# Matmul with batch normalization: the last tile's statistics aggregated in two steps, and its last chunk computed by two halves of rows

## The chip, the cores and the metric

One core of one Trainium2 chip. The metric is device time in microseconds (us), median of several executions. An execution more than 1.5% above the fastest one of the same kernel counts as slow and is left out.

## The reference, cut to what matters

```python
batch, m, k, n = 16, 512, 1024, 768          # x: (16, 512, 1024), weight: (1024, 768), float32
y = np.matmul(x, weight)
mean = np.mean(y, axis=(0, 1), keepdims=True)
var = np.var(y, axis=(0, 1), keepdims=True)
return (gamma * (y - mean) / np.sqrt(var + eps) + beta).astype(np.float32)
```

Every output column needs its mean and variance over all 8192 rows before any of it can be stored. The kernel splits the 768 columns into six tiles of 128 (nt) and the rows into 16 chunks of 512 (c). Tile 5 is the last. The "hole" below is the pause of about a microsecond between the last stores of tile 4 and the first of tile 5, in which the DMA engines, which carry the stores, have little to do.

## The kernel before

The pools, in the order in which they are laid out in on-chip memory (SBUF).

```python
singles = ctx.enter_context(tc.tile_pool(name="singles", bufs=1))
xtpool = ctx.enter_context(tc.tile_pool(name="xtpool", bufs=C - EARLY))      # xT tiles, at the end o_sb tiles
ypool = ctx.enter_context(tc.tile_pool(name="ypool", bufs=C + (NT - GA) * 2 + 1))
sqpool = ctx.enter_context(tc.tile_pool(name="sqpool", bufs=4))
# ... cut: ring, w_sb and others in singles
stats = singles.tile([P, NT, C, 6], f32)
msq = singles.tile([P, GA], f32)
mv = singles.tile([P, NT, 2], f32)
# ... cut: std, tmp, rstd, warm
```

The end of a tile: statistics of each chunk, one aggregation, scale and shift, then for each chunk normalize, transpose, copy out of PSUM, store.

```python
def bn(nt, c):
    i = c if nt >= GA else COLS.index(c)
    seq(nc.vector.bn_stats(stats[:, nt, i, :], py[nt, c]))

def finish(nt):
    one = slice(nt, nt + 1)
    seq(nc.vector.bn_aggr(mv[:, nt, :], stats[:, nt, :, :]))
    seq(nc.scalar.activation(std[:, one], mv[:, nt, 1:2], AF.Sqrt, bias=eps_sb, scale=1.0))
    # ... cut: tmp, rstd, scale, shift

def out_copy(nts, m0, eng, late=False):
    # ... cut
    if late:                                     # the last tile only
        o_sb = xtpool.tile([P, tiles, cols], f32, tag="xT")
    else:
        o_sb = piece(tiles * cols).rearrange("p (s n) -> p s n", n=cols)     # a piece of ring
    # ... cut

def store(nts, m0, tiles):                       # rows of 128 floats: 512 bytes each
    seq(nc.sync.dma_start(out_flat[m0:m0 + tiles * P, nts[0] * P:(nts[-1] + 1) * P].rearrange(
        "(s p) n -> p s n", p=P), ost.pop((nts, m0))))
```

`at(time, function, ...)` only puts the functions into an order. Each engine then runs its own list in that order.

## Time and profile before

| | before |
|---|---|
| time, median of 6 | 221.13 us (220.65 to 222.17) |
| span of the profiled execution | 218.9 us |
| last chunk's first matmul | 197.94 us |
| square root (statistics done) | 201.14 us |
| first store of tile 5 issued | 203.72 us |
| last store landed | 217.41 us |

The chain and the statistics' durations are in the prediction below.

From the timeline of the DMA queue that issues the stores, the second store of tile 5 (start, length):

```profile
204.21 1.13 SPq L358 DMA_DIRECT2D out_dram<-o_sb  x1
```

Its issue takes 1.13 us, where the later ones take about 0.53.

### The profile page before, as it was taken

Reading aid. Unit: us, or ns where it says so; the run is one execution under the profiler, and the core shown is the slowest. Engines: PE = TensorE matmul, PEld = TensorE weight load, DVE = VectorE, ACT = ScalarE, POOL = GpSimd, SP = SyncE. Lnnn points to the kernel's source line nnn. Section 1 sums busy time; section 2 is a strip of 40 time slices with the busy share of each in tenths; the row PEclk is TensorE's granted clock in tenths of the full one; section 3 lists DMA queues with packets and bytes.
Section 4 is the critical chain, followed back from the end, with each engine's and each line's share of the span. In section 5 each row is a group of like instructions: output and inputs, shape, how many; then the busy total and the mean of one; then the engine's idle time right before and its main releaser. Section 6 shows DMA issues by size and latency. Waiting matters only on the chain.

```text
span 218.9 us, 3417 instructions
## 1 busy us (share of the span) xinstructions
PE 198.5 (91%) x1154; PEld 105.2 (48%) x1170; DVE 155.7 (71%) x264; ACT 119.8 (55%) x220; POOL 134.0 (61%) x153
## 2 busy tenths in 40 slices
PE   7998999999999999999999979999999988995900
PEld 3453545454544555546555534444444545651900
DVE  3223788897978789998554287889989999745800
ACT  2001454554543566636666225776676887985850
POOL 8897595977765799935559103999899953000000
PEclk9999999999999999999999999999999999999795
DMA  5999999999999999990000000986769899999698
GB/s 60 175 204 190 194 196 196 197 196 196 194 191 197 195 196 196 198 189 10 0 4 0 0 0 14 340 308 257 269 258 360 295 353 334 346 346 347 201 345 244
DMA packets 70161, 43.75 MB, mean 200 GB/s; under 512 B 4096, under 2 KB 69632, under 8 KB 70144
## 3 DMA queue, kind: packets, MB, share of 16 engines
q0 software_dynamic: 34624, 18.36, 61.1%
q1 hardware_dynamic: 35520, 25.18, 35.7%
q8 instruction: 9, 0.15, 0.3%
q14 instruction: 8, 0.07, 0.1%
HBM read 36.71 MB, written 25.17 MB: 283 GB/s over the span
## 4 chain that ended last, share of the span: by engine, by line
PE 64%; DVE 10%; POOL 8%; DMA 6%; issue 4%; ACT 3%; ACTq 0%; DVEq 0%; POOLq 0%
PE y_ps L190 31%; PE y_ps L180 29%; POOL ring L280 6%; PE o_ps L340 3%; ACT o_sb L353 3%; DVE stats L299 3%; DMA w_sb<-in_weight_dram 3%; DVE ring L274 2%; DVE y_sb L324 2%; DMA ring<-in_x_dram 2%; POOL w_sb L143 2%; DMA out_dram<-ring 1%; POOL ring L156 1%; DVE mv L306 1%; PE a_ps L266 1%
## 5 line engine op out<-in xcount | busy, mean ns | idle before, releaser
L190 PE MATMUL y_ps<-xT_sb,w_sb 128*128 128x512 bf16 (+1 forms) x477 | 117.5, 381 | 2.6 <-DMA w_sb<-in_weight_dram 1.4
L190 PEld LDWEIGHTS <-w_sb 128*128 128x128 bf16 x492 | 46.7, 96 | 60.8 <-issue 3.1
L302 ACT CAST y_sb<-y_ps 128x512 bf16<-128x512 f32 x60 | 35.4, 590 | 53.3 <-DVE stats L299 51.4
L180 PE MATMUL y_ps<-w_sb,xT_sb 128*128 128x384 bf16 x384 | 63.4, 326 | 0.0
L299 DVE BATCH_NORM_STATS2 stats<-y_ps 128x6 f32<-128x512 f32 x60 | 40.6, 684 | 22.5 <-PE y_ps L190 22.3
L280 POOL TENSOR_TENSOR ring<-ring,sum 128x768 f32<-128x768 f32 x24 | 43.5, 1847 | 17.9 <-ACT sum L268 14.0
L156 POOL DMA_DIRECT2D ring<-in_x_dram x72 | 45.2, 633 | 11.7 <-DVE xT_sb L168 6.1
L180 PEld LDWEIGHTS <-xT_sb 128*128 128x128 bf16 x384 | 37.5, 98 | 25.6
L206 POOL TENSOR_TENSOR sum<-sum,sq_sb 128x384 f32<-128x384 f32 x38 | 38.0, 1000 | 18.0 <-ACT sq_sb L202 16.8
L168 DVE STREAM_TRANSPOSE xT_sb<-ring 128x1024 f32<-128x1024 f32 (+1 forms) x34 | 39.5, 1167 | 12.0 <-DMA ring<-in_x_dram 12.0
L340 PE MATMUL o_ps<-ident,y_sb 128*128 128x128 bf16 x240 | 37.3, 230 | 5.5 <-DVE y_sb L324 5.2
L209 DVE TENSOR_TENSOR sum<-y_ps,sum 128x384 f32<-128x384 f32 x48 | 26.1, 544 | 14.6 <-ACT sq_sb L202 13.8
L202 ACT ACTIVATE sq_sb<-y_ps 128x384 f32<-128x384 f32 x48 | 23.4, 492 | 14.9 <-PE y_ps L180 11.4
L215 ACT CAST y_sb<-y_ps 128x384 bf16<-128x384 f32 x48 | 22.9, 476 | 7.5 <-DVE sum L209 7.3
L353 ACT CAST ring<-o_ps 128x1024 f32<-128x1024 bf16 (+1 forms) x24 | 22.5, 960 | 4.9 <-PE o_ps L340 2.5
L340 PEld LDWEIGHTS <-y_sb 128*128 128x128 bf16 x240 | 20.6, 104 | 9.1 <-DVE y_sb L324 7.3
L274 DVE TENSOR_TENSOR ring<-y_sb,a_ps 128x768 f32<-128x768 bf16 x24 | 22.3, 938 | 0.2 <-PE a_ps L266 0.2
L324 DVE TENSOR_SCALAR y_sb<-y_sb,scale,shift 128x512 bf16<-128x512 bf16 x43 | 17.3, 457 | 0.0
L319 ACT ACTIVATE y_sb<-y_sb,shift,scale 128x512 bf16<-128x512 bf16 x17 | 13.3, 813 | 0.1
L149 PE MATMUL idle_ps<-idle_sb 128*128 128x512 bf16 x37 | 9.8, 429 | 1.2 <-DVE idle_sb L100 1.2
L353 ACT CAST o_sb<-o_ps 128x512 f32<-128x512 bf16 x16 | 7.9, 679 | 1.2 <-PE o_ps L340 1.2
L149 PEld LDWEIGHTS <-idle_sb 128*128 128x128 bf16 x38 | 4.0, 108 | 6.4 <-issue 1.9
(45 smaller groups left out, 35.9 us busy)
## 6 DMA issues: line engine op xcount, KB each, us to landing
ring<-in_x_dram POOLq DMA_DIRECT2D x56, 256.0 KB, 8.5
out_dram<-ring SPq DMA_DIRECT2D x32, 384.0 KB, 2.9
out_dram<-ring SPq DMA_DIRECT2D x16, 512.0 KB, 5.9
out_dram<-o_sb SPq DMA_DIRECT2D x16, 256.0 KB, 3.3
ring<-in_x_dram POOLq DMA_DIRECT2D x16, 128.0 KB, 5.2
w_sb<-in_weight_dram POOLq DMA_DIRECT2D x8, 96.0 KB, 4.6
w_sb<-in_weight_dram POOLq DMA_DIRECT2D x4, 192.0 KB, 5.4
gamma_sb<-in_gamma_dram SPq DMA_DIRECT2D x6, 0.5 KB, 4.8
```

What stands on the lines that cost most here:

```text
L156: seq(nc.gpsimd.dma_start(x_bf[32 * i:32 * i + 32], src[:, :, KQ * i:KQ * (i + 1)]))
L168: seq(nc.vector.transpose(dst[:, half, :, jw0:jw1], src[:, :, jw0:jw1]))
L180: seq(nc.tensor.matmul(y_ps, xT[c][:, jw, s * P:(s + 1) * P, e], w_sb[:, jw, e, 0:NA], start=(jw == 0 and e == 0), stop=(jw == JW - 1 and ...
L190: seq(nc.tensor.matmul(y_ps, w_sb[:, jw, e, nt * P:(nt + 1) * P], xT[c][:, jw, q0 * QR:q1 * QR, e], start=(jw == 0 and e == 0 and q0 == 0) ...
L206: seq(eng.tensor_add(acc, acc, py.pop(("sq", c, s))))
L209: seq(nc.vector.tensor_add(sum1, py["row", c, s][:, 0:NA], sum1))
L274: seq(nc.vector.tensor_mul(o_sb, yrow[c][:, s:s + 2], aff[0][:, None, :].to_broadcast([P, 2, NA]),))
L280: seq(nc.gpsimd.tensor_add(o_sb, o_sb, sum1[:, None, :].to_broadcast([P, 2, NA])))
L299: seq(nc.vector.bn_stats(stats[:, nt, i, :], py[nt, c]))
L302: seq(nc.scalar.copy(y(nt, c), py.pop((nt, c))))
L340: seq(nc.tensor.transpose(dst, src, ident))
L353: seq(nc.scalar.copy(o_sb, src))
```

## The change

Intent: shorten what stands between the last matmul and the first store of tile 5. The statistics of chunks 0 to 13 become one triple (count, mean, sum of squares) while TensorE still works. The last chunk is computed as two halves of 256 rows, so that the first half is measured while the second is computed.

```diff
     stats = singles.tile([P, NT, C, 6], f32)
+    fin = singles.tile([P, 21], f32)
     msq = singles.tile([P, GA], f32)
@@ (in bn)
+        if (nt, c) == (NT - 1, C - 2):
+            seq(nc.vector.bn_stats(fin[:, 3:9], py[nt, c]))
+            return
@@
+    def sum_up():
+        seq(nc.vector.memset(fin[:, 0:1], float((C - 2) * CH)))
+        seq(nc.vector.bn_aggr(fin[:, 1:3], stats[:, NT - 1, 0:C - 2, :]))
+        seq(nc.vector.tensor_scalar(
+            fin[:, 2:3], fin[:, 2:3], float((C - 2) * CH), None, op0=ALU.mult))
+
+    def mm_half(q):
+        y_ps = psum.tile([P, CH], f32, tag="b")
+        py["half", q] = y_ps[:, 0:QR]
+        # ... cut: the 8 matmuls of mm, on 256 rows
+
+    def bn_half(q):
+        seq(nc.vector.bn_stats(fin[:, 9 + 6 * q:15 + 6 * q], py["half", q]))
+
+    def keep_half(q):
+        seq(nc.scalar.copy(y(NT - 1, C - 1)[:, q * QR:(q + 1) * QR], py.pop(("half", q))))
@@ (in finish)
-        seq(nc.vector.bn_aggr(mv[:, nt, :], stats[:, nt, :, :]))
+        src = stats[:, nt, :, :] if nt < NT - 1 else fin
+        seq(nc.vector.bn_aggr(mv[:, nt, :], src))
@@ (in the loop that orders the chunks)
+            if (nt, c) == (NT - 1, C - 1):
+                for q in range(QPC):
+                    at(pe, mm_half, q)
+                    pe += 0.9
+                    at(pe + 0.2, bn_half, q)
+                    at(pe + (0.4 if q == 0 else 1.0), keep_half, q)
+                at(pe - 2.4, sum_up)
+                continue
```

## The prediction

> **What bounds the kernel now.** I began with the page's second part, the span in 40 slices, to see what is busy at the end, and then took each stretch by itself.
>
> ```profile
> PE   7998999999999999999999979999999988995900
> DVE  3223788897978789998554287889989999745800
> ACT  2001454554543566636666225776676887985850
> ...
> GB/s 60 175 204 190 194 196 196 197 196 196 194 191 197 195 196 196 198 189 10 0 4 0 0 0 14 340 308 257 269 258 360 295 353 334 346 346 347 201 345 244
> ```
>
> TensorE is full until about 200 us, then it dips once and is idle after some 208 us. From slice 26 on the output stores keep the DMA engines near 345 GB/s, with one hole, the 201 of slice 38. The change touches only the last 128 columns of the output (tile 5), of which nothing can be stored before their mean and variance are known. So the stretch to read is the hole, from 198 to 206 us. The chain of work that ended last gives it step by step (columns: start us, length us, what):
>
> ```profile
> 197.04 2.72 PE y_ps L190 x12
> 199.79 0.71 DVE stats L299
> 200.52 0.60 DVE mv L306
> 201.14 0.30 ACT std L307
> 201.47 0.17 DVE rstd L311
> 201.66 0.16 DVE scale L312
> 201.82 0.14 DVE shift L313
> 201.99 0.42 DVE y_sb L324
> 202.46 0.62 PE o_ps L340 x4
> 203.11 3.78 ACT o_sb L353 x8
> ```
>
> This is a serial tail: last matmul, statistics of the last chunk (0.71), aggregation of all 16 chunks (0.60), square root and three tiny operations, first normalization, four transposes, first copy out of PSUM. The first store of tile 5 is issued at 203.72 us in the timeline. Whatever shortens the front of this chain should bring the first store, and the 15 behind it, forward. After that the stores set the time: 16 of 256 KB are 4.19 MB, and at the 346 GB/s that the windows of 1 us show from 206 to 217 us they need 12.1 us; the copies on ScalarE come every 0.48 us, faster than a store's 0.76 us. The same windows show the DMA engines around the hole (columns: stretch, its length, busy time of each engine, granted TensorE clock, DMA share, GB/s):
>
> ```profile
> 201.00:202.00 1.00, 0.00 (x0) 0.00 (x0) 0.73 (x6) 0.77 (x2) 0.00 (x0) 1.00 1.15 346
> 202.00:203.00 1.00, 0.54 (x6) 0.54 (x7) 1.00 (x4) 0.00 (x0) 0.00 (x0) 0.65 0.83 250
> 203.00:204.00 1.00, 1.00 (x12) 1.00 (x11) 1.00 (x5) 0.89 (x2) 0.00 (x0) 0.50 0.16 39
> ```
>
> Tile 4's stores run out at about 202.7 us, so there is a whole microsecond with hardly a transfer before the first new store is issued. An earlier first store lands in an empty queue.
>
> **What the Trainium skill says.** "TensorE: Matmul & The Clock Gate", section "Back-to-back issue gap", gives a spacing of N/2.4 + 2.5 ns for one matmul of N columns behind another when the clock is full, and warns that weight loads can raise it for small N. The trace is near it: eight matmuls of 512 columns take 1.81 us here (197.94 to 199.75), 0.227 us each instead of 0.216. Matmuls of 256 columns are in this kernel already, in its first chunk; in the timeline they start at 13.35, 13.57, 13.80 and 14.03 us with two to a step, so 0.113 us each against a stated 0.109. Two halves cost what one whole costs. The same page, section "What's actually happening", has the array's clock halved after an idle window of about 3.4 us that runs freely. The trace agrees: the clock is 0.50 from 202.3 to 205.7 us, 3.4 us, after the pause of 2.71 us in PE. "VectorE: DVE Perf Modes", section "The TRN2 errata", makes an operation a fixed cost plus one cycle per element at 0.96 GHz. For the statistics this fits: 512 elements are 0.533 us, and 0.700 us are measured, a fixed 0.167 us. "PSUM — Partial Sum Buffer", section "PSUM bank collisions", says no two engines may use one bank at once; the halves get a bank each, so measuring the first need not stop the second's matmuls. No page gives a duration for the two batch-norm operations; those come from the trace.
>
> **The change part by part.** The aggregation is in the trace in two sizes (ns: least, median, most):
>
> ```profile
> L236 DVE BATCH_NORM_AGGREGATE mv<-stats x3: 205/205/245, 126.5 to 126.8; 128x2 f32<-128x24 f32 x3
> L306 DVE BATCH_NORM_AGGREGATE mv<-stats x3: 575/587/589, 150.9 to 200.5; 128x2 f32<-128x96 f32 x3
> L299 DVE BATCH_NORM_STATS2 stats<-y_ps x60: 652/688/700, 19.8 to 199.8; 128x6 f32<-128x512 f32 x60
> ```
>
> - Removed from the chain: the aggregation over 96 values. It becomes one over 21 (a triple for 14 chunks, two for chunk 14, two for each half). From (587 - 205)/(96 - 24) = 5.3 ns a value, 21 values are 205 - 3 x 5.3 = 189 ns. Saved: 587 - 189 = 0.40 us.
> - Removed from the chain: half of the last statistics. 256 fewer elements at 0.96 GHz, so 0.70 becomes 0.70 - 0.267 = 0.43 us. Saved: 0.27 us.
> - Moved: statistics of the first half. They run while TensorE computes the second half: ready at about 197.94 + 0.95 = 198.89 us, done at 199.32, and the second half ends at 199.79. Beside other work, cost nothing.
> - Added on TensorE: eight more matmuls, of half the width. 16 x 0.113 = 1.81 us, as before. Cost 0.0 us.
> - Added on VectorE, ahead of chunk 14's statistics: a memset of one column (59 ns for such a one), an aggregation over 84 values (205 + 60 x 5.3 = 523 ns) and a multiplication of one column (169 ns for a like one), 0.75 us and some 0.1 us between them. They stand in order after chunk 13's statistics (195.67 to 196.37) and before those of chunk 14 at 197.98; VectorE idled 1.61 us there waiting for TensorE. They fit, with 0.7 us over. Cost 0.
> - Added on ScalarE: one copy of 512 becomes two of 256. The first runs near 199.4 us, before the square root needs the engine at about 200.47; the second comes after the square root as the whole one did (201.34 to 201.90), and is done long before the first o_sb copy. Cost 0.
> - Not changed: square root to first copy, as many steps of the same size; 16 stores of the same size; everything before 195 us.
>
> Sum: 0.40 + 0.27 = 0.67 us. The square root should start at 201.14 - 0.67 = 200.47, the first o_sb copy at 202.44, the first store at 203.05, 0.35 us after the queue ran empty. The whole end then shifts by the same amount: 221.04 - 0.67 = 220.4 us, or 0.3%.
>
> **The rivals.**
> - The hole is filled by the transfers: tile 4's stores still occupy the queue when tile 5's arrive, so the earlier start is worth nothing. Against it are the 39 GB/s in 203 to 204 us and the queue's end at 202.7; the shift of 0.67 is smaller than the 1.0 us between that end and the first issue. If it were so, the time would stay at 221.0. A part of it may be true: the second store's issue took 1.13 us where the others took about 0.53, and if the issues are irregular in another way the gain could shrink or grow by 0.3 us.
> - Weight loads bind with narrow matmuls: 16 loads of 96 ns stand under 16 steps of 113 ns, with little room, and the skill's page warns of it. At 0.13 us a step the last chunk would take 2.08 us, 0.27 us more, which leaves 0.4 us: 220.6. Against it is the spacing of the 24 narrow matmuls at 13 us, which changed weights each time as well.
> - The aggregation has a larger fixed cost, or costs by the number of distinct statistics in some other way. Then only the half of the statistics is gained, 0.27 us: 220.8. The two sizes measured speak against it.
> - The clock: the pause in PE shrinks from 2.71 to about 2.04 us. The halved clock made the first four transposes last 0.62 us where four at full clock take about 0.4. If the shorter pause, or merely another position of the free-running window, keeps the clock, 0.2 us more are gained: 220.2. The window from 205.7 to 209.1 was 2.0 us busy of 3.4 and did not lower the clock; the one from 198.9 to 202.3 was 0.85 us busy and did. After the change the least busy window would hold 1.4 us. Between the two; I give it one in three, and later transposes don't matter, since the copies and then the stores are slower.
> - Slower: only if the new VectorE work delayed chunk 14's statistics, or a half waited for a bank. The eight tiles ahead of the second half's bank were freed more than a microsecond before, by the order of the program. I see no way past 0.3 us.
>
> **Range and chances.** The three times of before spread from 220.65 to 222.17, a longer tail above than below, which is larger than the effect. Mechanisms alone give 220.2 to 221.0; with a median's noise of some 0.4 us on both sides I take 219.7 to 221.3. Faster by over 2% would need 4.4 us, six times what the chain offers; slower by as much has no mechanism. Within 2%: 0.97.
>
> **What would show it.** In the profile after, right if: the last statistics are of 128x256 and last 0.43 us; the last aggregation is of 128x21 and lasts about 0.19 us; the square root starts about 0.65 us after the last statistics start (1.35 before); the last chunk's 16 matmuls take 1.8 us; the aggregation over 84 values ends before 197.5 us with chunk 14's statistics still waiting for TensorE; the first store is issued 5.1 us after the last chunk's first matmul (5.8 before); from there to the end of the span it stays 15.2 us. The prediction is wrong if that last length grows by what the first shrank, or if the statistics' two pieces are not shorter in proportion.

## More of the kernel before

Of the windows of before, here are one from the start of tile 5's stores and the stretch that is mostly stores (columns: stretch, its length, busy time and instructions of PE, PEld, DVE, ACT, POOL, granted TensorE clock, DMA share, GB/s):

```profile
204.00:205.00 1.00, 1.00 (x13) 1.00 (x11) 1.00 (x5) 1.00 (x3) 0.00 (x0) 0.50 0.40 120
...
208.00:217.00 9.00, 0.00 (x0) 0.00 (x0) 0.00 (x0) 3.04 (x7) 0.00 (x0) 0.75 1.15 345
```

In the first the stores have begun and move only 120 GB/s; the 345 GB/s at the end of the second line are the rate at which tile 5 leaves.

## The result, and the profile after

The changed kernel takes 223.15 us (median of 6, 222.83 to 223.74), before 221.13. The ratio is 1.0089, with a 95% interval of 1.0064 to 1.0114. A ratio here is the mean time of one kernel's fast runs over that of the other's fast runs of the same rounds, so not quite the ratio of the medians. The kernel became slower by 0.9%, where a gain of 0.3% was predicted. It stays within 2%, to which the prediction gave 0.97, but lies outside its range of 219.7 to 221.3 us.

The chain of work that ended last, of the changed kernel (start us, length us, what):

```profile
199.26 1.83 PE y_ps L317 x16
201.11 0.45 DVE fin L324
201.58 0.26 DVE mv L335
201.86 0.30 ACT std L336
...
202.71 0.43 DVE y_sb L353
203.18 0.41 PE o_ps L369 x4
203.62 3.97 ACT o_sb L382 x8
```

Count from the last chunk's first matmul, 199.26 us here and 197.94 before. The square root comes at 2.60 us for 3.20. The first o_sb copy comes at 4.36 for 5.17, and the first store is issued at 4.97 (204.23 us) for 5.78. The front of the chain is 0.8 us shorter, a little more than was predicted, but not for the predicted reason alone: 0.60 of it comes from the statistics (0.67 predicted), and 0.21 from the first four transposes, which found the clock full in this trace (0.41 us for 0.62). The instructions that write or read `fin` (columns: engine, operation, count: ns least/median/most, first and last start) show how:

```profile
L324 DVE BATCH_NORM_STATS2 fin<-y_ps x2: 433/433/433, 200.2 to 201.1; 128x6 f32<-128x256 f32 x2
...
L308 DVE BATCH_NORM_AGGREGATE fin<-stats x1: 534/534/534, 197.7 to 197.7; 128x2 f32<-128x84 f32 x1
...
L335 DVE BATCH_NORM_AGGREGATE mv<-fin x1: 249/249/249, 201.6 to 201.6; 128x2 f32<-128x21 f32 x1
```

So far the prediction holds. Now the windows of the changed kernel, at the start of the stores and in the stretch of stores alone:

```profile
203.00:204.00 1.00, 0.82 (x11) 0.62 (x12) 1.00 (x4) 0.38 (x1) 0.00 (x0) 1.00 1.15 348
204.00:205.00 1.00, 1.00 (x16) 0.71 (x13) 1.00 (x5) 1.00 (x3) 0.00 (x0) 1.00 0.56 167
205.00:206.00 1.00, 1.00 (x16) 0.70 (x13) 1.00 (x5) 1.00 (x3) 0.00 (x0) 1.00 0.87 258
...
208.00:217.00 9.00, 0.43 (x6) 0.23 (x4) 0.00 (x0) 3.55 (x8) 0.00 (x0) 0.72 0.99 288
```

The last column tells where the time went. Tile 4's stores still ran at 348 GB/s, but tile 5's run at 288 where before had 345. They are the same 16 stores of 256 KB with the same rows of 512 bytes. At 345 GB/s their 4.19 MB take 12.2 us, at 288 they take 14.6. The DMA share falls with the rate, from 1.15 to 0.99: the single packets last about as long (from 208 to 216 us 26.4 ns in the mean before, 27.3 now), but they follow each other more slowly. From the first store's issue to the end of the span it takes 17.2 us (204.23 to 221.47) in place of 15.2.

Two more differences are in the trace. The second store's issue, 1.13 us before, is short now:

```profile
204.72 0.44 SPq L387 DMA_DIRECT2D out_dram<-o_sb  x1
```

And a 16-KB packet on the DMA queue that the profile calls "q8 instruction" has moved. In before's packet records the last one starts at 203.6 us, in the hole. In the changed kernel it starts at 200.2 us, while tile 4's stores still fill the DMA engines. The DMA view of the changed kernel for 198 to 202 us has it, and that of before for the same stretch has none:

```profile
q1 hardware_dynamic: 2691, 1.35, 113.0%
q8 instruction: 1, 0.02, 1.5%
```

Last, the profiled execution was already 1.3 us later when the last chunk began. This part is no effect of the change that can be shown. The first statistics of the kernel start at 19.8 us in before's trace and at 20.9 in the changed kernel's, but two executions of one and the same kernel (after_moved below) have 21.3 and 19.5.

### The profile page after: what moved, and what is told of

Its sections match the earlier page's. It is cut to its first block, busy times and chain, and to the rows that moved or that the text cites. A ratio compares the mean times of both kernels' runs of the same rounds, so it can differ in the third digit from the quotient of the medians.

```text
span 221.5 us, 3438 instructions
## 1 busy us (share of the span) xinstructions
PE 199.8 (90%) x1162; PEld 105.0 (47%) x1178; DVE 156.3 (71%) x268; ACT 119.9 (54%) x221; POOL 134.4 (61%) x153
## 4 chain that ended last, share of the span: by engine, by line
PE 63%; DVE 10%; POOL 8%; DMA 6%; issue 4%; ACT 3%; ACTq 0%; DVEq 0%; POOLq 0%
PE y_ps L191 30%; PE y_ps L181 28%; POOL ring L281 6%; PE o_ps L369 3%; ACT o_sb L382 3%; DMA w_sb<-in_weight_dram 3%; DVE stats L303 2%; DMA ring<-in_x_dram 2%; DVE ring L275 2%; DVE y_sb L353 2%; POOL w_sb L144 2%; DMA out_dram<-ring 1%; POOL ring L157 1%; PE y_ps L317 1%; PE a_ps L267 1%
## 5 line engine op out<-in xcount | busy, mean ns | idle before, releaser
L191 PE MATMUL y_ps<-xT_sb,w_sb 128*128 128x512 bf16 (+1 forms) x469 | 115.8, 382 | 2.6 <-DMA w_sb<-in_weight_dram 1.6
L191 PEld LDWEIGHTS <-w_sb 128*128 128x128 bf16 x484 | 46.2, 96 | 59.4 <-issue 2.6
L330 ACT CAST y_sb<-y_ps 128x512 bf16<-128x512 f32 x59 | 34.8, 590 | 54.2 <-DVE stats L303 52.3
L303 DVE BATCH_NORM_STATS2 stats<-y_ps 128x6 f32<-128x512 f32 x58 | 39.2, 684 | 19.9 <-PE y_ps L191 19.7
L169 DVE STREAM_TRANSPOSE xT_sb<-ring 128x1024 f32<-128x1024 f32 (+1 forms) x34 | 39.5, 1168 | 13.6 <-DMA ring<-in_x_dram 13.5
L369 PEld LDWEIGHTS <-y_sb 128*128 128x128 bf16 x240 | 19.1, 97 | 9.7 <-DVE y_sb L353 6.5
L150 PE MATMUL idle_ps<-idle_sb 128*128 128x512 bf16 x37 | 11.2, 473 | 1.2 <-DVE idle_sb L100 1.2
```

Of the source, the lines that this page charges most:

```text
L169: seq(nc.vector.transpose(dst[:, half, :, jw0:jw1], src[:, :, jw0:jw1]))
L191: seq(nc.tensor.matmul(y_ps, w_sb[:, jw, e, nt * P:(nt + 1) * P], xT[c][:, jw, q0 * QR:q1 * QR, e], start=(jw == 0 and e == 0 and q0 == 0) ...
L330: seq(nc.scalar.copy(y(nt, c), py.pop((nt, c))))
L369: seq(nc.tensor.transpose(dst, src, ident))
```

## The experiments

**Theory.** `fin` takes 84 bytes, for which the layout gives 96: in the compiled program msq moves from 61728 to 61824, and everything behind it moves as far. The o_sb tiles, which lie in the pool behind singles, move from 61952, a multiple of 256, to 62048, 96 bytes past one. `ring`, from which tile 4 is stored, lies in front of `fin` and did not move. So the stores of tile 5 alone became slower. The page "DMA: Bandwidth & Descriptors" of the Trainium skill, section "How a descriptor splits into AXI transactions", says that a transfer is cut into transactions at 256-byte boundaries and counts their cost in beats of 32 bytes. By that, a row of 512 bytes costs 16 beats where it starts on a boundary and 19 where it starts 96 bytes behind one: 345 x 16/19 is an estimate of 291 GB/s.

**Rivals.** The new work itself disturbs the stores (TensorE at full clock, other order of the copies). Or any move of the pools costs something in the engines' reads and writes.

To compare traces without the varying start, the tables count from the last chunk's first matmul. It is taken as the last statistics' start less 1.85 us, which is what the chains of both kernels have. "Landed" is the end of the last packet of the last store.

**pad96**: the kernel before, and nothing but a tile that is never used.

```diff
+    pad = singles.tile([P, 24], f32)
     msq = singles.tile([P, GA], f32)
```

> The kernel before with nothing added but an unused 96-byte tile in front of msq, which puts the o_sb tiles 96 bytes past a 256-byte boundary, where the change put them. Address theory: a 512-byte row of a store then takes 19 beats of 32 bytes in place of 16, so the last stores run at 346 x 16/19 = 291 GB/s (287 measured in the changed kernel) and the time is about 2.1 us over before, some 223.2. Rival, that the changed work itself (halves, earlier statistics, full clock at the transposes) slows the stores: 346 GB/s and 221.1 us, as before.

Measured: 223.95 us, ratio 1.0125 (1.0085 to 1.0166). The window of 208 to 217 us of this kernel:

```profile
208.00:217.00 9.00, 0.31 (x6) 0.14 (x3) 0.00 (x0) 3.45 (x8) 0.00 (x0) 0.79 0.98 286
```

The statistics are as in before and the stores as slow as in the changed kernel. The rate falls without any of the new work.

**after_moved**: the changed kernel with `fin` behind all other pools, so every other tile has before's address.

```diff
+    finpool = ctx.enter_context(tc.tile_pool(name="finpool", bufs=1))
-    fin = singles.tile([P, 21], f32)
+    fin = finpool.tile([P, 21], f32)
```

> The changed kernel with fin in a pool of its own behind all others, so that every other tile has the address it had before. Address theory: stores at 346 GB/s again, and the gain of the shorter statistics (0.6 to 0.8 us) is left: 220.4 us, ratio 0.997. Rival, the changed work slows the stores: 287 GB/s and 223.1 us. If the late start of the early part (weights landed 1.1 us later in the changed kernel's trace) belongs to the changed program and not to the run, 1 us more than the first figure.

Measured: 221.17 us, ratio 0.9989 (0.9959 to 1.0018). The same window:

```profile
208.00:217.00 9.00, 0.61 (x8) 0.34 (x7) 0.16 (x1) 3.74 (x8) 0.00 (x0) 0.77 1.15 345
```

All of the new work is there and the rate is whole again. The loss is gone, but the time does not show a gain either: the interval includes the 0.997 that was expected and includes 1.

**pad256 and pad224**: as pad96, with `[P, 64]` and `[P, 56]`.

> The kernel before with an unused 256-byte tile: o_sb at a multiple of 256 that is no multiple of 512. Address theory with blocks of 256 bytes: 16 beats a row, 346 GB/s, 221.1 us. If boundaries of 512 bytes are what counts, or any move of the pools costs: under 346 GB/s and about 2 us more.

Measured: 221.54 us, ratio 1.0011 (0.9977 to 1.0044), 346 GB/s. A move by 256 bytes shows no cost.

```profile
208.00:217.00 9.00, 1.57 (x20) 1.00 (x18) 1.12 (x4) 4.70 (x10) 0.00 (x0) 0.81 1.15 346
```

> The kernel before with an unused 224-byte tile: o_sb 224 bytes past a 256-byte boundary. Beats theory: 8 + 8 + 7 = 23 beats a row, 346 x 16/23 = 241 GB/s, some 4.7 us over before: 225.8 us. Rival, any start off the boundary costs the same: 287 GB/s and 223.2 us.

Measured: 223.43 us, ratio 1.0096 (1.0061 to 1.0130), 286 GB/s.

```profile
208.00:217.00 9.00, 0.51 (x8) 0.23 (x5) 0.05 (x1) 3.64 (x8) 0.00 (x0) 0.72 1.04 286
```

The count of beats, which would give 23 for 16, is wrong for this: 224 bytes past the boundary cost what 96 do.

**pad64 and pad128**: as pad96, with `[P, 16]` and `[P, 32]`, one execution each (state unknown).

> The kernel before with an unused 64-byte tile: o_sb starts 64 bytes past a 256-byte boundary. If what counts is a boundary of 256 bytes, as the skill's page has it, the last stores run at 286 GB/s as with 96 and 224 bytes; if a boundary of 64 bytes is enough, at 346 GB/s.

> The kernel before with an unused 128-byte tile: o_sb starts 128 bytes past a 256-byte boundary. If a boundary of 256 bytes counts: 286 GB/s. If 128 is enough: 346 GB/s. Together with the 64-byte run this finds the size of the boundary.

Measured: 285 and 286 GB/s, and single times of 222.76 and 224.31 us. The boundary is 256 bytes: of six offsets, 0 and 256 gave 345 and 346 GB/s, and 64, 96, 128 and 224 all gave 285 to 286.

**only_o_sb**: all pools where they were in before, only the o_sb tiles 96 bytes further inside their buffers.

```diff
-            o_sb = xtpool.tile([P, tiles, cols], f32, tag="xT")
+            o_wide = xtpool.tile([P, 24 + tiles * cols], f32, tag="xT")
+            o_sb = o_wide[:, 24:].rearrange("p (s n) -> p s n", n=cols)
```

> The padded kernels moved four pools at once (xT, y and sq tiles as well). Here every pool stays where it was in before, and only the 16 o_sb tiles start 96 bytes into their buffers. If the source address of the stores alone is the cause: 286 GB/s in the last stage, the last store lands 21.4 to 21.9 us after the last chunk's first matmul (19.2 to 19.5 with aligned tiles), time about 223.4 us, ratio 1.011. If it is the address of what the engines read and write beside the stores (y_sb, xT_sb, sq_sb): 346 GB/s and 221.2 us.

Measured: 224.01 us, ratio 1.0111 (1.0057 to 1.0165).

```profile
208.00:217.00 9.00, 1.65 (x21) 1.48 (x19) 0.57 (x2) 4.15 (x9) 0.00 (x0) 0.69 0.98 286
```

The address of the o_sb tiles alone does it. The copies that fill these tiles moved with them, but last no longer (median 0.67 us for 0.68 before), so it is the stores' reading that became slower.

**Where the gain of the front went.** after_moved issues its first store as early as the changed kernel (4.97 us), but its last store landed only 0.1 to 0.4 us sooner than in the aligned kernels with before's program (19.11 for 19.47 and 19.19). Its windows at the very end, and the packet records, show why. Of the last store's 16 completions 14 lie within 0.15 us, at 217.5 to 217.6 us, one follows at 217.95, and one comes at 218.56:

```profile
217.00:218.00 1.00, 0.00 (x0) 0.00 (x0) 0.00 (x0) 0.00 (x0) 0.00 (x0) 0.50 0.66 198
218.00:219.00 1.00, 0.00 (x0) 0.00 (x0) 0.00 (x0) 0.00 (x0) 0.00 (x0) 0.50 0.04 12
```

At 345 GB/s one of 16 DMA engines moves 22 GB/s, which is also what the records show between 217.95 and 218.56 us. So one engine was late (the packet records do not name engines; this is read from the rate). Before has such an engine too: from 203 to 204.5 us its packet records show 21 to 23 packets of 512 bytes in every half microsecond, where 336 are moved when all are busy. There it catches up in the hole, and at the end all 16 finish within 0.15 us (217.27 to 217.41).

The suspect was the instruction fetch. The page "Runtime: NRT & Kernel Launch" of the Trainium skill, section "Instruction fetch mechanics", says that instructions are fetched in blocks of 16 KB (256 instructions) by a DMA queue of the engine's own, and calls the cost "mostly hidden". The changed kernel has 16 more rows in TensorE's program (8 matmuls and 8 weight loads: 2332 for 2316 in the compiled programs; the expectations below count 2330 for 2314), so that a block's end is reached earlier. The idle matmuls at the start (`WAKE = 30`, two rows each) can shift it back, or shift it in the kernel before.

**moved_wake22**: after_moved with `WAKE = 22`, as many rows as before.

> The changed kernel with fin behind all pools (no address moved) and with 8 fewer of the idle matmuls at the very start (WAKE 22 for 30), so that TensorE's instruction stream has the length it had before (2314 rows; the change had made it 2330). Instruction-fetch theory: the last 16-KB fetch of TensorE's instructions, which fell at 200.0 to 200.2 us in both traces with the longer stream, falls back into the hole at 203 to 204 us; the second o_sb store's issue again takes 1.0 to 1.3 us, the 16 DMA engines finish the last store within 0.2 us of each other (1.0 us in after_moved), and the time from the last chunk's first matmul to the last store's landing is 0.5 to 0.8 us less than before's 19.5 us; time 220.4 us, ratio 0.997. Rival, the early front itself makes one DMA engine lag: the lag of 1 us stays and the ratio stays at 0.999.

Measured: 221.43 us, ratio 0.9990 (0.9956 to 1.0023). The fetch is back in the hole, at 204.7 us (4.9 us after the first matmul), and the second store's issue is long again:

```profile
205.28 1.25 SPq L388 DMA_DIRECT2D out_dram<-o_sb  x1
```

All 16 engines finish within 0.15 us, and the last store landed at 18.77 us, 0.56 us sooner than the mean of before and pad256 (19.33). This is what the theory expected of the trace; the whole time is too coarse to show it, for the ratio is the 0.999 of the rival, and its interval holds the theory's 0.997 too.

**before_wake38**: the kernel before with `WAKE = 38`, 16 rows more.

> The kernel before with 8 more idle matmuls at the start (WAKE 38), nothing else: TensorE's stream is 2330 rows as in the change. Instruction-fetch theory: the last fetch moves from 203.6 us to about 200 us, among tile 4's stores; the second o_sb store's issue then takes about 0.45 us in place of 1.13, and one DMA engine finishes about 1 us after the others. The time stays within 0.5 us of before (221.1), as the quicker start of the stores and the lag offset each other. Rival, the fetch has nothing to do with either: second issue 1.0 to 1.3 us, all engines finish within 0.2 us.

Measured: 220.99 us, ratio 0.9978 (0.9933 to 1.0023). The fetch moved to 198.9 us, and with nothing else changed the second issue became short:

```profile
204.68 0.44 SPq L358 DMA_DIRECT2D out_dram<-o_sb  x1
```

The late engine that was expected at the end did not come: all 16 finish within 0.15 us, and the last store landed at 18.77 us. So the fetch among the stores is not enough for the lag; here tile 4's rest still had until 204.6 us to drain before new data came. The paragraphs behind the table come back to this.

**agg_only and halves_only**: one part of the change each, `fin` behind all pools (the last chunk whole and an aggregation over 15 values; or the halves and one aggregation over 102 values).

```diff
 agg_only, in bn:
+        if nt == NT - 1 and c >= C - 2:
+            i = 3 + 6 * (c - (C - 2))
+            seq(nc.vector.bn_stats(fin[:, i:i + 6], py[nt, c]))
+            return
 halves_only, in bn:
+        if nt == NT - 1:
+            seq(nc.vector.bn_stats(fin[:, 6 * c:6 * c + 6], py[nt, c]))
+            return
```

> Only the early aggregation, with fin behind all pools: the last chunk stays whole, its statistics are of 512 columns, the last aggregation is over 15 values. From the aggregations of 21 (249 ns) and 24 values (205 to 245 ns) and of 96 (587 ns) it should last 0.20 to 0.23 us, so the square root starts 0.36 us sooner after the last chunk's first matmul than in before (2.84 for 3.20 us). TensorE's stream is as long as before, so the last instruction fetch stays in the hole at about 203.5 us with a second o_sb issue of 1 us or more. Stores at 346 GB/s. Time 220.7 us, ratio 0.998.

Measured: 221.06 us, ratio 0.9985 (0.9926 to 1.0044). The square root starts at 2.84 us, the aggregation takes 223 ns.

> Only the halves, with the statistics of all chunks kept in one tile behind all pools and one aggregation over 102 values: the last statistics 433 ns for 700, the aggregation about 0.62 us for 0.59; the square root 0.23 us sooner than in before (2.97 us after the last chunk's first matmul). TensorE's stream has 16 rows more, so the last fetch comes about 200 us and the second o_sb issue takes about 0.45 us. Stores at 346 GB/s.

Measured, one execution (state unknown): 220.77 us; the square root at 2.97 us, statistics of 432 ns and an aggregation of 616 ns.

The two parts of the front are 0.36 and 0.23 us, together 0.59, and the whole change has 0.60.

**after_moved_again**: the same kernel as after_moved.

> The same kernel as after_moved, for one more trace of its end: if the one DMA engine that finished 1.0 us after the 15 others belongs to this order of fetch and stores, it does so again; if it was chance, all finish within 0.2 us and the last store lands 18.2 us after the last chunk's first matmul instead of 19.1.

Measured, one execution (state unknown): 220.47 us. One engine is late again, 217.16 us against 216.43 to 216.60 for the others. The last store landed at 18.76 us.

All traces in one table (us from the last chunk's first matmul):

| kernel | o_sb past 256 | PE rows added | last fetch | square root | first issue | second issue's length | GB/s, stores alone | landed |
|---|---|---|---|---|---|---|---|---|
| before | 0 | 0 | 5.6 | 3.20 | 5.78 | 1.13 | 345 | 19.47 |
| pad256 | 0 | 0 | 5.7 | 3.20 | 5.57 | 1.06 | 346 | 19.19 |
| pad64 | 64 | 0 | 5.4 | 3.20 | 5.56 | 0.89 | 285 | 21.45 |
| pad96 | 96 | 0 | 5.5 | 3.21 | 5.72 | 0.98 | 286 | 21.66 |
| only_o_sb | 96 | 0 | 5.5 | 3.20 | 5.57 | 1.23 | 286 | 21.75 |
| pad128 | 128 | 0 | 5.5 | 3.20 | 5.79 | 1.06 | 286 | 21.76 |
| pad224 | 224 | 0 | 5.6 | 3.20 | 5.57 | 1.36 | 286 | 21.92 |
| changed | 96 | 16 | 0.9 | 2.60 | 4.97 | 0.44 | 288 | 20.70 |
| after_moved | 0 | 16 | 0.6 | 2.60 | 4.97 | 0.43 | 345 | 19.11 |
| after_moved_again | 0 | 16 | 0.2 | 2.60 | 4.97 | 0.43 | 346 | 18.76 |
| moved_wake22 | 0 | 0 | 4.9 | 2.60 | 4.97 | 1.25 | 345 | 18.77 |
| before_wake38 | 0 | 16 | 0.2 | 3.21 | 5.57 | 0.44 | 346 | 18.77 |
| agg_only | 0 | 0 | 5.2 | 2.84 | 5.21 | 1.14 | 345 | 18.94 |
| halves_only | 0 | 16 | 0.3 | 2.97 | 5.34 | 0.43 | 346 | 18.74 |

(The rate is that of 208 to 217 us; of after_moved_again, which ends earlier, of 207 to 216.)

Read the table in three groups. Five kernels with before's work and o_sb off the boundary landed at 21.71 us in the mean, two on the boundary at 19.33: the address costs 2.4 us. With o_sb on the boundary and the fetch in the hole, a front shorter by 0.36 or 0.60 us lands 0.39 or 0.56 us sooner than that mean, and 0.25 or 0.42 us sooner than pad256, which had the full clock at the first transposes as these two did: most of it is passed on, as far as one trace of each can tell. With the fetch moved out of the hole, three traces land at 18.74 to 18.77 us and one at 19.11, whether the front is as before or shorter by 0.23 or 0.60 us: there a shorter front showed no further gain. In every kernel whose last fetch fell into the hole the second issue took 0.89 to 1.36 us, and in every one whose fetch fell before it 0.43 or 0.44.

The last store's 16 completion packets show where the gain went. With the fetch before the hole and o_sb on the boundary, all but the last one or two of them have come 13.2 us after the first store's issue, in each of the four traces: counted from the first matmul, at 18.77 us in before_wake38, 18.54 in halves_only, and 18.18 and 18.20 in the two of after_moved. They pass a shorter front on in full. The very last comes at 18.77, 18.74, 19.11 and 18.76 us: in three of four it does not move with the front, and before_wake38 shows no lag because there the others are as late. With the fetch in the hole all 16 come together, but 13.6 to 13.8 us after the first issue (before, pad256, agg_only, moved_wake22): the long second issue goes with a loss of 0.4 to 0.6 us for all engines.

## Why the prediction was wrong

- **The bound and the hole: right.** The front of the chain sets when the stores begin, and the stores set the rest.
- **The statistics' halves: right.** 0.43 us predicted, 0.433 measured.
- **The aggregation: a little short.** 189 ns predicted, 249 measured. The line through 24 and 96 values used the quickest of three run in a row; the first of those took 245. The aggregations of the last tile, over 15, 21, 84, 96 and 102 values, took 223, 249, 534, 587 and 616 ns, which lie within 2 ns of 155 ns + 4.5 ns a value. The front became 0.60 us shorter by the statistics, not 0.67.
- **The eight more matmuls: right in TensorE's time** (16 took 1.83 us), wrong in what else they do: their 16 rows of program move the last instruction fetch out of the hole.
- **VectorE's and ScalarE's added work: right**, it lies in idle time (the aggregation over 84 values took 534 ns for 523 and ended before chunk 14's statistics could begin). The square root started 0.75 us after the last statistics for 0.65 predicted.
- **The clock** happened to stay full at the first transposes of the changed kernel's trace (0.41 us for 0.62), as the fourth rival had it. This was luck: with before's longer pause it also stayed full there in five traces (pad256, pad64, pad224, only_o_sb, before_wake38: first issue 5.56 or 5.57 for 5.78 us), and with the shorter pause it still halved in four of six, only later (at 203.8 to 204.4 us). The prediction's "the trace agrees" holds for the length of the halved stretch, 3.4 us; the 3.4 us before it were not idle but 0.85 us busy, as the prediction itself counts further down.
- **The step that failed** is the last of the list, "Not changed: square root to first copy, as many steps of the same size; 16 stores of the same size", and with it "the whole end then shifts by the same amount". The diff's own line `fin = singles.tile([P, 21], f32)` was read as an operand and not as 96 bytes in front of three pools. The 16 stores have the same size but start 96 bytes past a 256-byte boundary, and run at 288 GB/s for 345. From the first issue to the end it takes 17.2 us and not 15.2.
- **The first rival**, that transfers swallow the gain, was put too simply. The queue as a whole is empty for a microsecond, but one of the 16 DMA engines still drains tile 4 in it. For that engine there is hardly a hole. (With the fetch before the hole the last completion stayed near 18.75 us in three of four traces, whatever the front gained, as it would for an engine without a hole. That it belongs to the engine that drained tile 4 late is not shown.)
- **A small reading:** slices 26 to 32 of the prediction's GB/s row run from 257 to 360, not near 345. Nothing rests on it.

The sum from the landing times: an address worth +2.38, a front of -0.60, and a rest of -0.41 make 20.70 - 19.33 = +1.37 us. Of the rest, 0.07 is the clock at the first transposes (the five off the boundary issued their first store at 5.64 us in the mean, so 0.67 later than the changed kernel, of which the front is 0.60). The other 0.34 lies between first issue and landing (15.73 us for a mean of 16.07), where the quick second issue is the likely cause. The interval of the ratio, 1.0064 to 1.0114 of 221.13, is 1.4 to 2.5 us with a middle of 2.0. What lies between 1.4 and 2.0 stays open. The early part varies by 2.1 us between traces, and the six executions can have had it later by chance, but nothing here shows that.

Open too: how a fetch makes the second store's issue long, why one DMA engine is behind at all, and why the last completion came 0.35 us later in one trace of after_moved (19.11) than in the other (18.76). No version was shown to beat the kernel before: after_moved, moved_wake22, before_wake38 and agg_only lie 0.1 to 0.2% below it, with intervals that include 1. Their landing times, 0.2 to 0.6 us sooner, are a few traces' evidence.

## What to carry to other kernels

A new tile, however small, moves what is laid out behind it: put it last, or check that the tiles which DMAs read keep their 256-byte boundary (shown here for stores with rows of 512 bytes). When a step before a stretch of stores is shortened, ask of each DMA engine and not of the queue whether it was idle. For effects under 1% compare positions in the trace from a late common point, since the start alone varied by more than the effect.

## What the Trainium skill lacked or had wrong

- "DMA: Bandwidth & Descriptors", section "How a descriptor splits into AXI transactions": the boundary of 256 bytes is confirmed, the cost in beats is not. For stores of 512-byte rows it gives 18, 19, 20 and 23 beats at offsets of 64, 96, 128 and 224 bytes, for 16 on the boundary; measured are 285, 286, 286 and 286 GB/s for 345 to 346, one cost for all. The same section's splitting gives three transactions for two at each of these offsets, so a cost by transactions would fit; no run tests that. The page's rules for kernel authors do not say to keep a store's source on the boundary; here it was worth 2.4 of 221 us.
- "Runtime: NRT & Kernel Launch", section "Instruction fetch mechanics": blocks of 16 KB fit the packets of q8 (those of the other instruction queue, q14, are of 8 KB). "Mostly hidden" leaves out that they compete with the stores: where the fetch falls among tile 4's stores, these fall from about 340 packets in half a microsecond to 317 to 321 for a microsecond, by about one engine's share of 21; a fetch in the hole goes with a store's issue of 0.89 to 1.36 us in place of 0.43 to 0.44, and 16 rows of program are enough to move it.
- No page that was read gives a time for the batch-norm operations. Statistics out of PSUM took 433 ns for 256 and 698 for 512 elements; the aggregation 223, 249, 534, 587 and 616 ns for 15, 21, 84, 96 and 102 values, about 155 ns and 4.5 ns a value (three over 24 values in a row were quicker than that, 245, 205 and 205 ns).
